# The first product of the last MLP as seven block products with sums of blocks

## The chip, the cores and the metric

The kernel runs on one NeuronCore of a Trainium2 chip. The metric is the device time of one execution in microseconds (us), as the median of several executions. The engines are named as in the profile: PE (TensorE, matmuls), PEld (its weight loads), DVE (VectorE), ACT (ScalarE), POOL (GpSimd), and SP, whose queue issues the loads.

## The reference, cut to what matters

One transformer block on 1024 tokens of width 1024: a mixer of two kinds of sparse attention, cross-attention to a memory, and an MLP, each with a residual sum. All is float32. What the change touches is the MLP:

```python
def _sq_relu_mlp(h, w_ff_in, w_ff_out):
    return jnp.square(jax.nn.relu(h @ w_ff_in)) @ w_ff_out
...
        x = x + _sq_relu_mlp(_rms_norm(x, norm3_g[l]), w_ff_in[l], w_ff_out[l])
```

`w_ff_in` is 1024 x 4096 and `w_ff_out` 4096 x 1024.

## The kernel before, in words

The tokens are eight tiles of 128. The kernel projects them, then runs the attention of each tile while other work (projection of the second half, the memory's keys, the dense part of finished tiles) fills PE's gaps; `together`, `beside` and `merge` interleave these streams by the numbers that they yield. After the attention only dense work is left: `between` (output projection, cross-attention) for tiles 4 and 5 in the pool `dn` and for tiles 6 and 7 in the pool `d2`, merged, and then `mlp(d2, 4, 4, x2s)` for tiles 4 to 7, alone. The functions write the instructions in program order, with tiles from rings of fixed depth (`RINGS`) and PSUM banks by tag (`PSUMS`: S 2, PT 2, PV 1, D 2, M 1). A scheduler then orders the instructions of each engine by a timeline of its own, and each engine runs its queue in that order.

A float32 product is done as three fast ones (type float32r): each operand is split into a high part (a rounding copy) and a low part (the rest), and high x high, low x high and high x low are summed in PSUM. Weights are split by `split_w` (lines 240 to 249): the high part on ACT, the low part on POOL or DVE, two of three on POOL in this stage (`PLAN_TAIL`). `mm` (line 218) records every matmul, so the profile shows all under L218.

`mlp` (line 988) first reads x2 of tiles 4 and 5 back from DRAM (L993), while tiles 6 and 7 are still in SBUF. `norm_T2` (line 289) squares and sums a tile (L293), gets the scale (L229, L231), norms it in halves (L297), transposes it on PE (L274) and splits it into xh and xl (L235, L236). The MLP then runs in eighths, 512 features each (`f4`). In an eighth, for two blocks of 256 features (`f2`), four loads of 256 KB (L254) are split, and each 128 features get 8 x 3 matmuls over all 512 tokens into one bank of S; relu and square follow on ACT (L1020, L1021), the split of the result h on POOL (L1023, L1024). The second product takes, for each half of the output columns (`c`), four loads of 256 KB and for each token tile 4 x 3 matmuls of 512 columns, also into S; DVE adds the result to x2 (L899), and in the last eighth it is stored. The pools `wraw`, `whi` and `wlo` of `d2` have 3, 6 and 6 buffers, `h` has 8.

## Time and profile before

| what | us |
|---|---|
| median of three runs (1859.41 to 1865.53) | 1861.02 |
| the profiled execution | 1861.12 |
| its span on the core | 1859.0 |
| first matmul of the last MLP, after the span's start | 1492.83 |
| last residual sum starts | 1855.28 |
| PE busy, whole span | 1729.4 |

The granted clock of PE has a mean of 0.973 over the span. In a timeline row the first number is the start, the second the duration, then engine, line, operation, tiles and shape; brackets hold the idle time ahead of it and what ended that. In a row of grouped instructions, the numbers behind the bar are the total busy time in us and the mean of one in ns, then the idle time ahead of them. A matmul's own duration is no measure of its cost, since the next one starts before it ends; the steps from start to start are.

### The profile page before, as it was taken

Reading aid. Unit: us, or ns where it says so; the run is one execution under the profiler, and the core shown is the slowest. Engines: PE = TensorE matmul, PEld = TensorE weight load, DVE = VectorE, ACT = ScalarE, POOL = GpSimd, SP = SyncE. Lnnn points to the kernel's source line nnn. Section 1 sums busy time; section 2 is a strip of 40 time slices with the busy share of each in tenths; the row PEclk is TensorE's granted clock in tenths of the full one; section 3 lists DMA queues with packets and bytes.
Section 4 is the critical chain, followed back from the end, with each engine's and each line's share of the span. In section 5 each row is a group of like instructions: output and inputs, shape, how many; then the busy total and the mean of one; then the engine's idle time right before and its main releaser. Section 6 shows DMA issues by size and latency. Waiting matters only on the chain. (4 is left out here: it accounts for less than half of the span.)

```text
span 1859.0 us, 28028 instructions
## 1 busy us (share of the span) xinstructions
PE 1729.4 (93%) x9262; PEld 1467.8 (79%) x9262; DVE 934.9 (50%) x2353; ACT 1077.2 (58%) x2687; POOL 894.7 (48%) x1034
## 2 busy tenths in 40 slices
PE   5996999899989987899998999999898899999999
PEld 5995988678877776688886888888787778788787
DVE  4554766566773786466545565565333332222222
ACT  4444658898697678756984569975223233333332
POOL 2365557455451344466764766664111134444553
PEclk9998998999999998899999999999998999999999
DMA  8225413166226231121221221222773313222232
GB/s 198 71 86 163 98 35 99 65 212 178 90 86 193 88 83 42 46 70 56 77 77 57 67 72 60 64 71 93 241 249 109 116 63 97 91 91 91 91 98 101
DMA packets 180081, 187.50 MB, mean 101 GB/s; under 512 B 34657, under 2 KB 149089, under 8 KB 179937
## 3 DMA queue, kind: packets, MB, share of 16 engines
q1 hardware_dynamic: 172000, 175.23, 31.2%
q0 software_dynamic: 7936, 10.49, 2.1%
q8 instruction: 73, 1.20, 0.3%
q14 instruction: 72, 0.58, 0.1%
HBM read 164.69 MB, written 20.97 MB: 100 GB/s over the span
## 5 line engine op out<-in xcount | busy, mean ns | idle before, releaser
L249 POOL TENSOR_TENSOR wlo<-wraw,whi 128x512 fp32r<-128x512 f32 (+1 forms) x230 | 308.2, 1349 | 322.3 <-ACT whi L244 265.0
L244 ACT ACTIVATE whi<-wraw 128x512 fp32r<-128x512 f32 (+2 forms) x289 | 180.9, 628 | 251.8 <-PE psS L218 150.0
L218 PE MATMUL psD<-whi,xh 128*128 128x256 f32 (+1 forms) x704 | 192.7, 357 | 5.8 <-ACT whi L244 3.5
L218 PE MATMUL psD<-wlo,xh 128*128 128x256 f32 (+1 forms) x704 | 192.5, 354 | 0.8 <-DMA wlo<-in_w_in_dram 0.6
L218 PE MATMUL psD<-whi,h 128*128 128x512 f32 x512 | 177.1, 406 | 9.4 <-POOL h L1024 3.7
L236 DVE TENSOR_TENSOR pl<-psPT,ph 128x512 fp32r<-128x512 f32 (+1 forms) x232 | 141.8, 620 | 62.2 <-ACT ph L235 61.2
L218 PE MATMUL psS<-whi,h 128*128 128x512 f32 x512 | 162.0, 392 | 5.1 <-DVE b L899 5.1
L688 ACT ACTIVATE S<-S,mn 128x128 f32<-128x128 f32 (+7 forms) x192 | 142.8, 745 | 38.9 <-DVE mn L686 38.2
L235 ACT ACTIVATE ph<-psPT 128x512 fp32r<-128x512 f32 (+1 forms) x232 | 122.9, 541 | 57.7 <-PE psPT L703 50.0
L249 DVE TENSOR_TENSOR wlo<-wraw,whi 128x512 fp32r<-128x512 f32 (+1 forms) x59 | 59.4, 1007 | 175.5 <-ACT whi L244 171.8
L218 PEld LDWEIGHTS psD<-whi,xh 128*128 128x128 f32 x704 | 132.7, 195 | 17.2 <-ACT whi L244 3.9
L218 PEld LDWEIGHTS psD<-wlo,xh 128*128 128x128 f32 x704 | 133.6, 195 | 12.7 <-DMA wlo<-in_w_in_dram 1.0
L703 PE MATMUL psPT<-c_ident,S 128*128 128x128 f32 x816 | 133.9, 279 | 10.3 <-POOL S L693 4.7
L693 POOL TENSOR_SCALAR S<-S,sums,gi 128x640 f32<-128x640 f32 (+7 forms) x128 | 107.4, 850 | 68.2 <-DVE sums L691 59.2
L899 DVE TENSOR_TENSOR b<-psS,b 128x512 f32<-128x512 f32 (+1 forms) x80 | 50.0, 636 | 140.9 <-PE psS L218 140.8
L218 PEld LDWEIGHTS psD<-whi,h 128*128 128x128 f32 x512 | 95.8, 190 | 31.6 <-POOL h L1024 5.0
L218 PEld LDWEIGHTS psS<-whi,h 128*128 128x128 f32 x512 | 96.0, 188 | 29.4 <-DVE b L899 9.4
L218 PE MATMUL psS<-K,qh 128*128 128x384 f32 (+3 forms) x288 | 109.2, 383 | 6.6 <-DVE mn L686 2.6
L703 PEld LDWEIGHTS psPT<-c_ident,S 128*128 128x128 f32 x816 | 97.0, 142 | 20.8 <-POOL S L693 8.1
L899 DVE TENSOR_TENSOR b<-psD,b 128x512 f32<-128x512 f32 (+1 forms) x112 | 63.2, 572 | 87.6 <-PE psD L218 76.0
L218 PE MATMUL psD<-xh,wlo 128*128 128x512 f32 x256 | 102.1, 401 | 0.7 <-POOL wlo L249 0.7
L218 PE MATMUL psD<-wlo,h 128*128 128x512 f32 x256 | 102.3, 402 | 0.0
(299 smaller groups left out, 4643.7 us busy)
## 6 DMA issues: line engine op xcount, KB each, us to landing
wraw<-in_w_ff_in_dram SPq DMA_DIRECT2D x128, 256.0 KB, 2.8
wraw<-in_w_ff_out_dram SPq DMA_DIRECT2D x128, 256.0 KB, 2.7
whi<-in_w_out_dram SPq DMA_DIRECT2D x32, 256.0 KB, 5.3
wlo<-in_w_out_dram SPq DMA_DIRECT2D x32, 256.0 KB, 5.2
wraw<-in_w_in_dram SPq DMA_DIRECT2D x24, 256.0 KB, 3.7
q<-st SPq DMA_DIRECT2D x12, 512.0 KB, 2.6
qin<-q SPq DMA_DIRECT2D x44, 128.0 KB, 2.3
x<-in_x_dram SPq DMA_DIRECT2D x8, 512.0 KB, 5.2
```

What stands on the lines that cost most here:

```text
L218: te.matmul(o, a, b, start=start, stop=stop)
L235: s.activation(hi, src, AF.Copy)
L236: v.tensor_tensor(lo, src, hi, op=ALU.subtract)
L244: s.activation(hi, raw, AF.Copy)
L249: (v if l == "v" else g).tensor_tensor(lo, raw, hi, op=ALU.subtract)
L688: s.activation(S, S, AF.Exp, bias=low, scale=-1.0, accum_out=sums[:, hh:hh + 1])
L693: g.tensor_scalar(Ss[hh], Ss[hh], sums[:, hh:hh + 1], 1.0 if gate is None else gate[:, hh:hh + 1], op0=ALU.mult, op1=ALU.mult)
L703: te.transpose(p2[:, j, hh, :], S[:, (c + j) * P:(c + j + 1) * P], ident)
L899: v.tensor_tensor(dst, pt, dst, op=ALU.add)
```

## The change

The last call `mlp(d2, 4, 4, x2s)` becomes `mlp_seven`, with a pool `d3` of its own beside `d2`. The normed tokens, transposed, stand as a 2 x 2 array of blocks B[k][j]: half of the 1024 inputs (k) by half of the 512 tokens (j). The weights of 256 features are a 2 x 2 array A[i][k]: 128 features by half of the inputs. Where the plain way takes eight products of blocks, the new function takes seven, each 128 features x 512 inputs x 256 tokens, of sums of blocks (the Winograd form of Strassen's scheme). The seven sums of token blocks are made and split once (`operand`, R1 to R7); those of the weights for each 256 features (`weight_sum`, four of them; three of the seven are single blocks). Each product is 4 x 3 matmuls of 256 columns. Its results are summed by DVE out of PSUM into `sum` (lines 1138 to 1144 after the change), and relu and square then work on all four blocks at once; h is split as before.

Beside that: loads are 512 KB (L1117, L1159) through a ring of four `raw` tiles, which at first hold B; `whi` and `wlo` in `d2` get 13 buffers each in place of 6, `wraw` of `d2` goes; the second product uses banks of D, S and PT in turn in place of S alone; the MLP's weights are no longer loaded ahead of the raw tiles. The second product's matmuls, the weights' bytes and the stores are the same in number.

```diff
--- before.py
+++ after.py
@@ -37,7 +37,8 @@
     "p1": {"x4": 5, "st": 2, "relu": 4, "wraw": 4, "whi": 6, "wlo": 6, "c8": 4, "c4": 2, "kraw": 5, "pc": 2},
     "p2": {"x4": 3, "st": 1, "relu": 2, "whi": 4, "wlo": 4, "c8": 3, "c4": 1, "kraw": 4, "pc": 2},
     "dn": {"b4": 4, "h": 8, "relu": 2, "wraw": 2, "whi": 4, "wlo": 4},
-    "d2": {"b4": 4, "h": 8, "relu": 2, "wraw": 3, "whi": 6, "wlo": 6},
+    "d2": {"b4": 4, "h": 8, "relu": 2, "whi": 13, "wlo": 13, "sum": 2},
+    "d3": {"raw": 4, "T": 2, "ws": 4},
 }
 PSUMS = {"p1": {"D": 4, "M": 3, "C": 1}, "main": {"S": 2, "PT": 2, "PV": 1, "D": 2, "M": 1}}
 TAGS = {"p1": ("D", "M", "C"), "p2": ("D", "M", "D"), "dn": ("D", "M"), "d2": ("S", "PT")}
@@ -1044,6 +1045,137 @@
                                           x2[t][:, c * 512:(c + 1) * 512])
                     yield 2.6
 
+    def mlp_seven(pool, px, t0, x2s):
+
+
+        x2 = []
+        for t in range(4):
+            if t0 + t not in x2s:
+                x2s[t0 + t] = ring(pool, "b4", [P, DM])
+                nc.sync.dma_start(x2s[t0 + t], x2_dr[t0 + t])
+            x2.append(x2s[t0 + t])
+        add_to = residual_add(x2)
+        gb3 = gain2(pool, W["norm3_g"])
+        B = [[ring(px, "raw", [P, 4, 256]) for j in range(2)] for k in range(2)]
+        for t in range(4):
+            j, ts_ = t // 2, slice(t % 2 * P, t % 2 * P + P)
+            ss = small(pool, "nss", 1)
+            s.activation(ring(px, "T", [P, DM]), x2[t], AF.Square, accum_out=ss)
+            r = rsqrt_of(pool, ss, DM, 1, "n")
+            for k in range(2):
+                xn = ring(pool, "relu", [P, 512])
+                v.scalar_tensor_tensor(xn, x2[t][:, k * 512:k * 512 + 512], r[:, 0:1], gb3[k], op0=ALU.mult, op1=ALU.mult)
+                to_T(pool, xn, [B[k][j][:, :, ts_]], 4)
+            yield 1.0
+
+        R = {}
+
+        def operand(i, x):
+            R[i] = [px.tile([P, 4, 256], F32R, tag=f"R{i}{n}", name=f"R{i}{n}") for n in "hl"]
+            s.activation(R[i][0], x, AF.Copy)
+            v.tensor_tensor(R[i][1], x, R[i][0], op=ALU.subtract)
+
+        def minus(x, y):
+            d = ring(px, "T", [P, 4, 256])
+            v.tensor_tensor(d, x, y, op=ALU.subtract)
+            return d
+        operand(1, B[0][0])
+        t1 = minus(B[0][1], B[0][0])
+        operand(5, t1)
+        operand(2, B[1][0])
+        t2 = minus(B[1][1], t1)
+        operand(6, t2)
+        operand(3, B[1][1])
+        operand(4, minus(B[1][0], t2))
+        operand(7, minus(B[1][1], B[0][1]))
+
+        def split_of(x):
+            hi, lo = ring(pool, "whi", [P, 4, P], F32R), ring(pool, "wlo", [P, 4, P], F32R)
+            split_w(x, hi, lo)
+            return hi, lo
+
+        def product(pt, i, ws):
+            hi, lo = ws
+            xh, xl = R[i]
+            for k in range(4):
+                mm(pt, hi[:, k, :], xh[:, k, :], k == 0, False)
+                mm(pt, lo[:, k, :], xh[:, k, :], False, False)
+                mm(pt, hi[:, k, :], xl[:, k, :], False, k == 3)
+
+        def weight_sum(x, y, op):
+            d = ring(px, "ws", [P, 4, P])
+            v.tensor_tensor(d, x, y, op=op)
+            return d
+
+        for f4 in range(8):
+            hs = []
+            for f2 in range(2):
+                c0 = (f4 * 4 + f2 * 2) * P
+                raw = []
+                for k in range(2):
+                    x = ring(px, "raw", [P, 4, 256])
+                    nc.sync.dma_start(x, W["w_ff_in"][k * 512:k * 512 + 512, c0:c0 + 256].rearrange("(k p) n -> p k n", p=P))
+                    raw.append(x)
+                A = [[raw[k][:, :, i * P:(i + 1) * P] for k in range(2)] for i in range(2)]
+                w1 = split_of(A[0][0])
+                s1 = weight_sum(A[1][0], A[1][1], ALU.add)
+                w5 = split_of(s1)
+                w2 = split_of(A[0][1])
+                s2 = weight_sum(s1, A[0][0], ALU.subtract)
+                w6 = split_of(s2)
+                w3 = split_of(weight_sum(A[0][1], s2, ALU.subtract))
+                w7 = split_of(weight_sum(A[0][0], A[1][0], ALU.subtract))
+                w4 = split_of(A[1][1])
+
+                d = ring(pool, "sum", [P, 7, 256])
+                x, y, w, z = pst("S", [P, 2, 256]), pst("PT", [P, 2, 256]), pst("D", [P, 2, 256]), pst("PV", [P, 256])
+                c1 = small(pool, "c1", 256)
+                product(x[:, 0], 1, w1)
+                s.activation(c1, x[:, 0], AF.Copy)
+                product(x[:, 1], 5, w5)
+                product(y[:, 0], 2, w2)
+                product(y[:, 1], 6, w6)
+                v.tensor_tensor(d[:, 0:7:6], y, c1[:, None, :].to_broadcast([P, 2, 256]), op=ALU.add)
+                product(z, 7, w7)
+                v.tensor_tensor(d[:, 5], z, d[:, 6], op=ALU.add)
+                v.tensor_tensor(d[:, 3:5], x[:, 1:2].to_broadcast([P, 2, 256]), d[:, 5:7], op=ALU.add)
+                product(w[:, 0], 3, w3)
+                product(w[:, 1], 4, w4)
+                v.tensor_tensor(d[:, 1:3], w, d[:, 4:6], op=ALU.add)
+                s.activation(d[:, 0:4], d[:, 0:4], AF.Relu)
+                s.activation(d[:, 0:4], d[:, 0:4], AF.Square)
+                for i in range(2):
+                    r = d[:, 2 * i:2 * i + 2].rearrange("p a n -> p (a n)")
+                    hh, hl = ring(pool, "h", [P, 512], F32R), ring(pool, "h", [P, 512], F32R)
+                    g.tensor_scalar(hh, r, 1.0, 1.0, op0=ALU.mult, op1=ALU.mult)
+                    g.tensor_tensor(hl, r, hh, op=ALU.subtract)
+                    hs.append((hh, hl))
+                yield 9.7
+            for c in range(2):
+                gr = []
+                for k in range(0, 4, 2):
+                    raw = ring(px, "raw", [P, 2, 512])
+                    r0 = (f4 * 4 + k) * P
+                    nc.sync.dma_start(raw, W["w_ff_out"][r0:r0 + 256, c * 512:(c + 1) * 512].rearrange("(k p) n -> p k n", p=P))
+                    for i in range(2):
+                        hi, lo = ring(pool, "whi", [P, 512], F32R), ring(pool, "wlo", [P, 512], F32R)
+                        split_w(raw[:, i, :], hi, lo)
+                        gr.append((hi, lo))
+                for t in range(4):
+                    pt = pst(("D", "S", "PT")[t % 3], [P, 512])
+                    ts_ = slice(t * P, (t + 1) * P)
+                    for f in range(4):
+                        hh, hl = hs[f]
+                        wh, wl = gr[f]
+                        mm(pt, hh[:, ts_], wh, f == 0, False)
+                        mm(pt, hh[:, ts_], wl, False, False)
+                        mm(pt, hl[:, ts_], wh, False, f == 3)
+                    add_to(c, t, pt)
+                    if f4 == 7:
+                        nc.sync.dma_start(out[0, (t0 + t) * P:(t0 + t + 1) * P, c * 512:(c + 1) * 512],
+                                          x2[t][:, c * 512:(c + 1) * 512])
+                    yield 2.6
+
     def pe_stack():
         pe = p1.tile([P, 2, 32], F32R, tag="pe", name="pe")
         pe2 = ring(p1, "relu", [P, 2, 2, 64])
@@ -1111,7 +1243,9 @@
     rest = (w for w in rest if not isinstance(w, tuple))
     merge((rest, REST), (between(d2, 6, 2, x2s, True), 45.0))
     dn_pool.__exit__(None, None, None)
-    drain(mlp(d2, 4, 4, x2s))
+    d3_pool = tc.tile_pool(name="d3", bufs=1, reuse_waits="tile")
+    drain(mlp_seven(d2, d3_pool.__enter__(), 4, x2s))
+    d3_pool.__exit__(None, None, None)
     d2_pool.__exit__(None, None, None)
     ctx.close()
```

## The prediction, made before the changed kernel ran

> **What bounds the kernel now.** I read the page first, then the busy times of the last MLP alone, then the chain of work that ended last.
>
> ```profile
> PE 1729.4 (93%) x9262; PEld 1467.8 (79%) x9262; DVE 934.9 (50%) x2353; ACT 1077.2 (58%) x2687; POOL 894.7 (48%) x1034
> ```
> ```profile
> 1492.83:1855.28 362.45, 357.31 (x1538) 288.60 (x1536) 85.89 (x106) 113.95 (x187) 170.97 (x145) 1.00 0.29 92
> ```
> ```profile
> by line: PE psS L218 96.6%; DVE b L899 2.1%; PE psPT L274 0.3%; issue 0.2%
> ```
>
> The second row is one stretch: its ends (first and last matmul of the last MLP), its length, the busy us of PE, PE's weight loads, DVE, ACT and POOL with their instructions, then PE's granted clock and the DMA. TensorE is busy for 357.31 of the 362.45 us, VectorE for 85.89, ScalarE for 113.95 and GpSimd for 170.97. The chain (from 1492 us on) is nearly all matmuls of line 218, so here a matmul less is time won. A busy matmul is pipelined, so what one costs is the step from one start to the next:
>
> ```profile
> 1599.66 0.40 PE L218 MATMUL psS<-xh,whi 128*128 128x512 f32 x1
> ...
> 1606.39 0.40 PE L218 MATMUL psS<-xl,whi 128*128 128x512 f32 x1
> ...
> 1611.62 0.61 PE L218 MATMUL psS<-whi,h 128*128 128x512 f32 x2
> 1612.80 0.50 PE L218 MATMUL psS<-whi,h 128*128 128x512 f32 x1 [0.56 <-DVE b L899]
> 1613.13 0.39 PE L218 MATMUL psS<-wlo,h 128*128 128x512 f32 x1
> ...
> 1618.60 0.39 PE L218 MATMUL psS<-wlo,h 128*128 128x512 f32 x1
> ```
> ```profile
> PE psS L218 <- DVE b L899: 5.1, 10, 0.6
> ```
>
> First product: 29 steps in 6.73 us, 0.232 us each. Second product: 24 steps in 5.47 us, 0.228 us. Ten times PE waits for the residual sum to clear one of the two S banks: the pair at 1611.62 should be followed at about 1612.08 and is followed at 1612.80, so 0.72 us is lost, 7.2 us in all. An eighth of the MLP has 96 matmuls of each product: 22.3 + 21.9 = 44.2 us. Eight of them and the waits make 360.5 of the 362.45 us; the other 2.0 us is the slow beginning.
>
> **The change part by part.**
>
> *Matmuls.* One eighth had 2 x 2 x 8 x 3 = 96 products of 512 columns; now it has 2 x 7 x 4 x 3 = 168 of 256. The first projection of the kernel runs such 256-column matmuls, each with its own weight load, too:
>
> ```profile
> 28.92 0.28 PE L218 MATMUL psD<-whi,xh 128*128 128x256 f32 x1
> ...
> 30.10 0.29 PE L218 MATMUL psD<-wlo,xh 128*128 128x256 f32 x1
> ...
> 31.56 0.28 PE L218 MATMUL psD<-whi,xh 128*128 128x256 f32 x1
> ...
> 33.26 0.28 PE L218 MATMUL psD<-wlo,xh 128*128 128x256 f32 x1
> ```
>
> 10 steps in 1.18 us (0.118) and 15 in 1.70 us (0.113). I take 0.116, half of 0.232. So 168 x 0.116 = 19.5 us in place of 22.3: **2.78 us less per eighth, 22.3 us in all**; with 0.113 it is 26, with 0.118 it is 20. The 72 more weight loads cost nothing while they lie under the preceding matmul. Their price if that cover is gone is this row:
>
> ```profile
> L218 PEld LDWEIGHTS psS<-wlo,h 128*128 128x128 f32 x256 | 48.1, 188 | 9.7
> ```
>
> *Waits for the S bank.* The second product now rotates over D, S and PT, six banks in place of two: **7.2 us less**; the lower bound is nothing, if new waits stand there.
>
> *Work of the other engines.* Per eighth there are 22 weight splits in place of 16, 8 weight sums, 8 sums of products and 2 copies; relu, square and the split of h keep their size.
>
> ```profile
> L249 POOL TENSOR_TENSOR wlo<-wraw,whi 128x512 fp32r<-128x512 f32 x81 | 107.6, 1335 | 124.7 <-ACT whi L244 123.6
> ...
> L1024 POOL TENSOR_TENSOR h<-relu,h 128x512 fp32r<-128x512 f32 x32 | 44.5, 1391 | 1.8
> L249 DVE TENSOR_TENSOR wlo<-wraw,whi 128x512 fp32r<-128x512 f32 x41 | 43.1, 1050 | 164.1 <-ACT whi L244 164.1
> L899 DVE TENSOR_TENSOR b<-psS,b 128x512 f32<-128x512 f32 x63 | 42.5, 688 | 109.9 <-PE psS L218 109.9
> L1023 POOL TENSOR_SCALAR h<-relu 128x512 fp32r<-128x512 f32 x32 | 20.3, 634 | 62.1 <-ACT relu L1021 62.1
> ```
>
> GpSimd: 14.7 x 1.335 + 4 x (1.391 + 0.634) = 27.7 us. VectorE: 7.3 low parts and 8 weight sums at 1.05, 8 residual sums and 6 product sums at 0.69, 2 small ones at 0.42: 26.6 us. Both are below the 41.4 us of PE, so they bind only through order.
>
> *The order that may bind.* In the built program VectorE's queue puts s1 of the next but one weight block, and before it the four sums of the next block, ahead of the last product sum (after, line 1144). Behind that wait relu, square and GpSimd's two splits of h, which the second product needs. PE meanwhile has 36 matmuls on the two older h blocks: 36 x 0.228 = 8.2 us of cover after the seventh product, and 15 more to the last h. Counting from the start of the first block's products: its seventh ends at 9.7 us; the weights for the next block, whose raw tiles come free when the second product's first weights are split (9.5, behind the fourth product), are there one load of 4.5 us later, at 14 (its row stands below); eight two-input operations of VectorE at 1.05 and four reads of PSUM (10.9 us) end line 1144 at 25.0; relu and square of 1024 elements (1.06 each), then GpSimd's 0.63 + 1.39 + 0.63 + 1.39, end at 31.2. PE reaches that h at 19.5 + 51 x 0.228 = 31.1. Cover and chain are equal. I take 0.7 us of wait for each of the 7 later eighths, **5 us**; bounds 0 (VectorE alone, 0.69 an operation, below) and 2 each (14).
>
> *Start.* Before, the last residual sum and the first matmul stand 13.8 us apart:
>
> ```profile
> 1479.04 0.42 DVE L899 TENSOR_TENSOR b<-psS,b 128x256 f32<-128x256 f32 x1 [1.30 <-PE psS L218]
> 1479.09 1.06 ACT L293 ACTIVATE xh<-b 128x1024 fp32r<-128x1024 f32 x1 [0.28 <-PE psS L218]
> ...
> 1492.83 0.77 PE L218 MATMUL psS<-xh,whi 128*128 128x512 f32 x1
> ```
> ```profile
> L297 DVE SCALAR_TENSOR_TENSOR relu<-b,nr,h 128x512 f32<-128x512 f32 x8 | 5.9, 748 | 2.1 <-POOL nr L231 1.3 <-issue 0.7
> ...
> L899 DVE TENSOR_TENSOR b<-psS,b 128x256 f32<-128x256 f32 x6 | 2.5, 424 | 7.2 <-PE psS L218 7.2
> L249 DVE TENSOR_TENSOR wlo<-wraw,whi 128x512 fp32r<-128x512 f32 x2 | 1.4, 686 | 5.1 <-ACT whi L244 5.1
> ```
> ```profile
> wraw<-in_w_ff_in_dram SPq DMA_DIRECT2D x128, 256.0 KB, 2.8
> ...
> b<-in_x_dram SPq DMA_DIRECT2D x8, 512.0 KB, 4.5
> ```
>
> 256 more elements cost VectorE 0.264 us, so 1024 take about 1.22 (estimate). Now tiles 4 and 5 are normed and transposed inside the product before, where 16 transposes stand among the matmuls behind norms that wait for the tiles' loads; I let that delay it by 2.2 us, so its last sum ends at 1481.7. Then VectorE does in turn: norm of tile 6 (1.5), R1l and R2l (2.4), the wait for tile 7's scale and its norm (2.2); the transposes and copies of tile 7 end at 1488.3. Five operations of 1.22, the first low part (0.69) and two more of 1.22 follow: 1497.5. Only then is the raw tile free that holds the first tokens and is to take the second half of the first weights. The 512 KB load, at 5 us, lands at 1502.6; s1, its high part and its low part (0.7 + 0.63 + 1.34) let the second product go at 1505.3. The first has been done in the gap, the last six take 6 x 1.39 and a slow beginning: 1514.5. Less the 9.7 us that seven products take, that is as if they had begun at 1504.8, **12 us later** (bounds 9 and 16: a load of 2.8 us and no delay, or the double of both). In the first eighth the raw tiles for the second product come late too: the second block's splits end near 1516.5, the load behind them lands at 1521.5, and ScalarE's queue has seven splits, two of them from that load, ahead of the first relu. So relu and square end at 1524.9 and the first h's high part at 1525.5; GpSimd then has two low parts (to 1529.0) ahead of its low part, 1530.4. PE is there at 1514.5 + 9.7 = 1524.2 with ten matmuls that need high parts alone (2.3 us): it waits 1.3, then 2.6 us, and I add 0.6 for each of the two last h: **5 us** (bounds 2 and 8). The 2.0 us of slow beginning lies inside these waits.
>
> *The rest.* Rings of 13 instead of 6 for whi and wlo let the previous stage load earlier, and the MLP's own early loads are gone from that stretch of SP's queue; I cost this at nothing, since PE waits there for norms. If it frees or adds one wait for a load it is 2 us.
>
> **The sum**: -22.3 - 7.2 - 2.0 + 12 + 5 + 5 = -9.5 us. The profiled execution took 1861.1 us (span 1859.0), and the median of the runs shown is 1861.0. So 1851.6.
>
> **Rivals.**
>
> *All of it hidden* (start 9, first eighth 2, later none): -31.5 + 11 = -20.5, 1840.6. For it speaks that both side engines have a third of their time free. Chance 0.2.
>
> *Start and order cost it all* (16 + 8 + 1.5 x 7 = 34.5): 1864, no change. For it: the chain above has no slack. Chance 0.2.
>
> *VectorE and GpSimd in each other's way, slower.* The change triples VectorE's two-input work beside GpSimd.
>
> ```profile
> 1527.44 3.02 POOL L249 TENSOR_TENSOR wlo<-wraw,whi 128x512 fp32r<-128x512 f32 x2 [5.89 <-ACT whi L244]
> ```
> ```profile
> 1528.07 1.22 DVE L249 TENSOR_TENSOR wlo<-wraw,whi 128x512 fp32r<-128x512 f32 x1 [1.33 <-ACT whi L244]
> ```
>
> Alone such an operation took 0.686, here 1.22, and the two on GpSimd took 3.02 and not 2 x 1.29. Eight stand in the chain; if each took d, PE would wait 0.4 + 8 x (d - 1.05). The gain is gone at 2 us, d = 1.25; at 1.5 us it is 4 x 7 = 28 us, with 17 at the start 1875. Against it: the mean in this very stage is 1.05. Chance 0.12. The Trainium skill, Advanced Engine Details and Errata, VectorE Performance Modes, says the second SBUF port is shared and the two engines block each other; full blocking would make d 0.686 + 1.335 = 2.02 and the time about 1904, which the mean of 1.05 denies.
>
> *Weight loads come to light, slower.* 72 more per eighth at 0.188 us are 13.5 us, less 2.78 won: 8 x 10.8 = 86; with -9.2 and +22 for the rest about 1960. Against it: the 0.113 us steps, each with a load. Chance 0.03. In the Trainium skill, TensorE: Matmul & The Clock Gate, Part 3, The mechanism, a weight load overlaps running matmuls only when its row group differs; these use all rows, so by that rule this would be the case, and the rows above disagree with it.
>
> **How the numbers follow.** The forecast has 0.45, with a range of its own of 1845 to 1858. 0.3% is 5.6 us, about what a measurement of this kernel tells from no change. Faster (below 1855.4): 0.2 from the first rival and 0.40 of the forecast. Within: 0.05 of the forecast and 0.2. Slower: 0.15. The range of 1839 to 1867 leaves out the two slow rivals and a little below.
>
> **What would show it.** Right: 256-column matmuls 0.116 us apart; no wait of PE for line 899; the first product's second block beginning near 1504; eighths of 41.4 to 42.5 us from start to start. Wrong: steps above 0.124 us (the loads), PE waiting over 2 us per eighth for GpSimd's h with VectorE's weight sums above 1.25 us, or a start gap above 30 us.

## The result

The changed kernel takes 1849.8 us (median of four runs, 1849.0 to 1853.7), the kernel before beside it 1861.5 (1859.4 to 1865.5): a ratio of 0.9939, with a 95% interval of 0.9917 to 0.9961, or 7 to 15 us less. The forecast was 1851.6. The profiled execution took 1850.3 us, its span is 1848.6.

The busy times of the page, and then those of the stretch from the first to the last product of the last MLP (columns as in the row of before: ends, length, busy us of PE, weight loads, VectorE, ScalarE and GpSimd, PE's granted clock, DMA):

```profile
PE 1713.7 (93%) x9838; PEld 1489.5 (81%) x9838; DVE 1074.3 (58%) x2500; ACT 1110.4 (60%) x2726; POOL 957.7 (52%) x1066
```
```profile
1488.81:1844.80 355.99, 346.56 (x2112) 311.77 (x2112) 221.25 (x255) 146.01 (x225) 240.70 (x181) 0.97 0.31 99
```

PE's busy time falls by 15.7 us, VectorE's rises by 139.4, nearly all of it here (85.89 before). In this stretch PE was busy for all but 5.1 us before; now 9.4 are idle. The waits of PE for line 899 (now 900) are gone. From 1505 us on it waits for these, in all, times and longest:

```profile
PE psS L219 <- ACT c L1134: 3.7, 1, 3.7
PE psS L219 <- DVE sum L1141: 0.9, 3, 0.3
PE psD L219 <- DVE sum L1144: 0.3, 1, 0.3
```

The first is in the first eighth. Once this is over, PE's own rows in the fourth eighth's first block read:

```profile
1639.90 0.28 PE L219 MATMUL psD<-R3h,whi 128*128 128x256 f32 x1
...
1641.34 0.28 PE L219 MATMUL psD<-R4h,whi 128*128 128x256 f32 x1
...
1642.78 0.28 PE L219 MATMUL psS<-R1h,whi 128*128 128x256 f32 x1
```

Twelve steps in 1.44 us, twice: 0.120 us a step and not 0.116. An eighth's first product so takes 168 x 0.120 = 20.16 us, 2.11 less than the 22.27 of before, where 2.78 were forecast.

The start is the other end of the account. All of PE's waits from the first product to the second product of the first eighth:

```profile
1488.81 0.58 PE L219 MATMUL psS<-R1h,whi 128*128 128x256 f32 x1 [5.55 <-ACT whi L245]
1489.69 0.58 PE L219 MATMUL psS<-R1h,wlo 128*128 128x256 f32 x1 [0.30 <-DVE wlo L250]
1496.02 0.58 PE L219 MATMUL psS<-R5h,whi 128*128 128x256 f32 x1 [3.62 <-ACT whi L245]
1497.38 0.58 PE L219 MATMUL psS<-R5h,wlo 128*128 128x256 f32 x1 [0.25 <-POOL wlo L250]
1517.61 0.58 PE L219 MATMUL psS<-R5h,whi 128*128 128x256 f32 x1 [3.74 <-ACT c L1134]
```

The first block of products takes from 1488.81 to 1508.63, 19.8 us for 84 x 0.12 = 10.1 of work. VectorE's weight sums show why; here those of the first blocks, in order:

```profile
1494.62 0.69 DVE L1107 TENSOR_TENSOR ws<-raw 128x512 f32<-128x512 f32 x1 [0.24 <-DMA raw<-in_w_ff_in_dram]
1495.34 0.69 DVE L1107 TENSOR_TENSOR ws<-ws,raw 128x512 f32<-128x512 f32 x1
1496.07 1.80 DVE L1107 TENSOR_TENSOR ws<-raw,ws 128x512 f32<-128x512 f32 x1
1497.79 1.77 DVE L1107 TENSOR_TENSOR ws<-raw 128x512 f32<-128x512 f32 x1
```

The first waits for the weights. Those were loaded into tiles that the token blocks had held, and their two loads were issued only here:

```profile
1484.33 0.38 SPq L1117 DMA_DIRECT2D raw<-in_w_ff_in_dram  x1
...
1490.84 0.38 SPq L1117 DMA_DIRECT2D raw<-in_w_ff_in_dram  x1
```

The second landed at 1494.59, just ahead of the first sum. From 1496.05 on GpSimd works as well, and an operation of 0.69 us takes 1.8.

**How the kernels are compared below.** One profiled run differs from the next in the stages that all kernels share. So each trace is read from a mark, placed in the stage ahead of the last MLP: the twelve 128-column matmuls psS<-h.

```profile
1451.07 1.64 PE L219 MATMUL psS<-h 128*128 128x128 f32 x12
```

In the kernel before they begin at 1457.44. S2 is the first matmul of the second product in the second eighth, behind which six and a half even eighths follow; the end is that of the last matmul. All lengths in us:

| kernel | mark to S2 | S2 to end | together | median, its ratio to before |
|---|---|---|---|---|
| before | 104.3 | 293.5 | 397.8 | 1861 to 1863 |
| changed | 117.0 | 276.7 | 393.7 | 1849.8, 0.9939 |
| e1_banks | 103.7 | 286.2 | 389.9 | 1854.1, 0.9956 |
| e2_halves | 100.7 | 296.2 | 396.9 | 1858.4, 0.9984 |
| e3_eight | 101.7 | 290.9 | 392.5 | 1853.0, 0.9956 |
| e4_seventh_early | 115.4 | 276.1 | 391.4 | 1850.4, 0.9942 |
| e5_preload | 105.5 | 278.5 | 384.0 | 1846.4, 0.9902 |
| e6_rings | 104.4 | 292.3 | 396.7 | 1860.3, 0.9994 |
| e8_lows_dve | 109.6 | 274.4 | 383.9 | 1843.7, 0.9900 |
| e9_sums_twice | 122.7 | 307.1 | 429.8 | 1892.4, 1.0163 |
| e10_plain_block | 105.8 | 280.8 | 386.6 | 1848.3, 0.9925 |
| e11_plain_eighth | 101.9 | 278.6 | 380.4 | 1840.9, 0.9885 |
| e12_own_fourth | 101.1 | 278.0 | 379.1 | 1843.1, 0.9897 |
| e13_own_dve | 99.0 | 273.8 | 372.9 | 1831.9, 0.9835 |

The changed kernel gains 16.8 us in the even part and gives 12.7 back in the first eighth and what lies around it. The traces' sums and the medians differ by some microseconds, since the stretch ahead of the mark and the scatter of the runs are in the medians alone.

### The profile page after: what moved, and what is told of

The parts are those of the page before. It is cut to its first block, busy times and chain, and to the rows that moved or that the text cites. A ratio compares the mean times of both kernels' runs of the same rounds, so it can differ in the third digit from the quotient of the medians.

```text
span 1848.6 us, 29327 instructions
## 1 busy us (share of the span) xinstructions
PE 1713.7 (93%) x9838; PEld 1489.5 (81%) x9838; DVE 1074.3 (58%) x2500; ACT 1110.4 (60%) x2726; POOL 957.7 (52%) x1066
## 4 chain that ended last, share of the span: by engine, by line
PE 44%; issue 6%; DVE 6%; POOL 5%; DMA 5%; ACT 4%; SPq 1%; ACTq 0%; POOLq 0%; DVEq 0%
PE psD L219 23%; PE psS L219 11%; PE psPT L219 4%; PE psPV L219 3%; POOL wlo L250 3%; PE psPT L704 2%; DVE ws L1107 1%; DMA wraw<-in_w_ff_in_dram 1%; DMA raw<-in_w_ff_in_dram 1%; DMA wraw<-in_w_ff_out_dram 1%; ACT dmask L645 1%; POOL S L694 1%; DMA whi<-in_w_out_dram 1%; ACT whi L245 1%; POOL h L1025 0%
## 5 line engine op out<-in xcount | busy, mean ns | idle before, releaser
L219 PE MATMUL psD<-whi,h 128*128 128x512 f32 x768 | 266.0, 403 | 10.5 <-DVE b L900 3.6
L250 POOL TENSOR_TENSOR wlo<-wraw,whi 128x512 fp32r<-128x512 f32 x145 | 195.1, 1355 | 155.0 <-ACT whi L245 143.4
L219 PEld LDWEIGHTS psD<-whi,h 128*128 128x128 f32 x768 | 144.8, 191 | 44.2 <-DVE b L900 4.5
L900 DVE TENSOR_TENSOR b<-psD,b 128x512 f32<-128x512 f32 (+1 forms) x144 | 85.2, 598 | 130.0 <-PE psD L219 127.7
L219 PE MATMUL psD<-wlo,h 128*128 128x512 f32 x384 | 153.1, 400 | 0.0
L245 ACT ACTIVATE whi<-wraw 128x512 fp32r<-128x512 f32 (+1 forms) x161 | 100.0, 625 | 59.2 <-DMA wraw<-in_w_ff_in_dram 16.3
L245 ACT ACTIVATE whi<-raw 128x512 fp32r<-128x512 f32 x112 | 69.6, 628 | 106.7 <-PE psD L219 82.7
L250 POOL TENSOR_TENSOR wlo<-raw,whi 128x512 fp32r<-128x512 f32 x74 | 103.1, 1400 | 52.5 <-ACT whi L245 51.3
L232 POOL TENSOR_TENSOR nr<-nms,mhalf 128x1 f32<-128x1 f32 x26 | 14.9, 572 | 179.5 <-DVE nms L230 179.4
L219 PE MATMUL psD<-xh,wlo 128*128 128x512 f32 x256 | 101.9, 401 | 0.6 <-POOL wlo L250 0.6
L219 PE MATMUL psD<-xh,whi 128*128 128x512 f32 x256 | 100.8, 402 | 0.8 <-ACT xh L236 0.8
```

Source lines behind the costliest of these rows:

```text
L219: te.matmul(o, a, b, start=start, stop=stop)
L232: g.tensor_tensor(r, ms, mhalf[:, 0:1].to_broadcast([P, w]), op=ALU.pow)
L245: s.activation(hi, raw, AF.Copy)
L250: (v if l == "v" else g).tensor_tensor(lo, raw, hi, op=ALU.subtract)
L900: v.tensor_tensor(dst, pt, dst, op=ALU.add)
```

## Experiments

**The banks alone** (e1_banks, on the kernel before):

```diff
-                    pt = pst(TAGS[pool.name][0], [P, 512])
+                    pt = pst(("D", "S", "PT")[t % 3] if pool.name == "d2" else TAGS[pool.name][0], [P, 512])
```

> The kernel before, with one thing of the change alone: in the last MLP the second product's sums go over the banks D, S and PT in turn, where they all went to S and PT in the kernel before; the products stay as they were. Theory of the prediction: the ten waits of 0.72 us for the eviction of the bank S go and nothing takes their place, 7.2 us less than the kernel before (1861.5 - 7.2 = 1854.3, a ratio of 0.996). Rival: TensorE then waits for the next thing (a split of weights, h), and the time stays within 2 us of the kernel before. The two are told apart by the time and by PE's waits for line 900 after 1505 us.

1854.1 us, a ratio of 0.9956 (0.9939 to 0.9973), 7.9 less between mark and end, and PE waits for nothing after 1490 us. The prediction's 7.2 holds. By size this term of the change is two thirds of its whole result, and it needs no products by blocks. (In the kernel before all these sums go to S alone, not to S and PT as the expectation has it, and the line is 899.)

**The step of 256 columns** (e2_halves, on the kernel before):

```diff
-                    for k in range(8):
...
-                        mm(pt, wh[:, fs], xh[:, k, :], k == 0, False)
+                    wide = 256 if pool.name == "d2" else nt * P
+                    for j in range(0, nt * P, wide):
+                        cs = slice(j, j + wide)
+                        for k in range(8):
...
+                            mm(pt[:, cs], wh[:, fs], xh[:, k, cs], k == 0, False)
```

> The kernel before, with the last MLP's first product done in two halves of 256 columns, each with all its weight loads again: 192 matmuls of 256 columns for each eighth of the hidden units in place of 96 of 512, and nothing else. The prediction's price of 0.116 us a step gives 192 x 0.116 = 22.3 us, what 96 x 0.232 took: no change (within 2 us). The price read in the changed kernel, 0.120, if it belongs to every such step that has a weight load of its own, gives 192 x 0.120 = 23.0, 0.77 more in each eighth and 6.1 in all: 1867.6 (ratio 1.0033). If the 0.120 comes from something else of the change (other engines at work beside it), the steps here show 0.116. Rival, the loads exposed at 0.19 us each: 14 us more in each eighth, some 1975.

1858.4 us, 0.9984 (0.9972 to 0.9996). The 192 steps of an eighth take 22.67 us here (1627.57 up to the second product at 1650.24), 0.118 each: neither of the two prices. From S2 on it is 2.7 us slower than before, as 0.4 in each eighth says. That it is not slower in all comes from the start, 3.6 us shorter: matmuls of the first half of the tokens stand among the last transposes there. The loads are not exposed, and the time decides for neither theory: it is 3 us below the kernel before.

**Eight products in the new frame** (e3_eight, on the changed kernel):

```diff
-                w1 = split_of(A[0][0])
-                s1 = weight_sum(A[1][0], A[1][1], ALU.add)
...
+                ws = [[split_of(A[i][k]) for k in range(2)] for i in range(2)]
...
+                for i in range(2):
+                    x = pst(("S", "PT")[i], [P, 2, 256])
+                    for j in range(2):
+                        product(x[:, j], j, ws[i][0], True, False)
+                        product(x[:, j], 2 + j, ws[i][1], False, True)
```

> The changed kernel's frame (its pools, loads, order, blocks of 256 tokens, banks in turn) with the eight plain block products in place of the seven and without any of the sums of blocks: the same result by the ordinary rule. Steps per eighth 192 in place of 168, so by the step of 0.120 it loses 24 x 0.120 = 2.9 us in each eighth, 23.0 in all; it gains the waits of the eighths that the sums cause (5.6 us over the eight in the changed kernel) and part of the start (the sums of blocks before the first products, and the wait of 3.7 us in the first eighth: together 4 to 8). Theory: 1849.8 + 23.0 - 5.6 - 6 = 1861, between 1857 and 1868. Rival, that the sums of blocks eat the eighth product's worth and the gain came from the banks and the frame alone: 1850 or less.

1853.0 us, 0.9956 (0.9939 to 0.9973): below what the theory said, and not told apart from the changed kernel by the intervals. It is also above the rival's 1850. The trace tells why. From S2 on, where six first products lie, the seven products win 14.2 us over the eight (276.7 against 290.9), 2.4 in each eighth of the 2.9 that 24 steps of 0.120 are worth. Up to S2 they lose 15.3 (117.0 against 101.7), although two first products lie there and should win 5.8. So the sums cost 21 us up to there, where I had put 6, and that eats the whole gain.

**What the start waits for.** First, the operand that holds back the second weight load, made earlier (e4_seventh_early, on the changed kernel):

```diff
         t1 = minus(B[0][1], B[0][0])
         operand(5, t1)
+        operand(7, minus(B[1][1], B[0][1]))
```

> The changed kernel with the operand of the seventh product made right behind the first difference of blocks (a third buffer of T for it), so that the last reader of the blocks B, whose buffers the second weight load takes, is done earlier; all else is the same. Theory: the second block's load starts some 4 us earlier, the wait of 3.74 us for the raw split at 1517.6 and part of the gap before the second block go: 1849.8 - 3.7 = 1846, at best 1844. Rival: the loads already come in time for what VectorE and ScalarE can do there, the wait moves to the next split, and the time stays within 1.5 us of the changed kernel (1848.3 to 1851.3). It may cost up to 1 us where the first products wait one more operation for their operands.

1850.4 us, 0.9942 (0.9927 to 0.9957): the rival. The wait for line 1134 is as long as it was, and so is the one before the first product:

```profile
1492.00 0.58 PE L219 MATMUL psS<-R1h,whi 128*128 128x256 f32 x1 [5.80 <-ACT whi L245]
...
1520.30 0.58 PE L219 MATMUL psS<-R5h,whi 128*128 128x256 f32 x1 [3.73 <-ACT c L1134]
```

Of the loads for the second product, the second landed 3.4 us earlier than in the changed kernel (counted from the mark), but the third, whose splits the copy of line 1134 stands behind, only 0.8.

Then the first weights loaded early, into tiles that are free (e5_preload, on the changed kernel):

```diff
+        early = []
+        for k in range(2):
+            x = ring(pool, "sum", [P, 7, 256])[:, 0:4]
+            nc.sync.dma_start(x, W["w_ff_in"][k * 512:k * 512 + 512, 0:256].rearrange("(k p) n -> p k n", p=P))
+            early.append(x)
```

> The changed kernel with one thing else: the weights of the very first block are loaded at the head of the last MLP into the two buffers of 'sum', which are free there, and not into buffers of the blocks B that the operands have to leave first. From the last residual sum of the stage before to the first product of the second eighth the kernel before took 60.4 us (1479.04 to 1539.45), the changed kernel 71.05 (1475.57 to 1546.62). Theory of the prediction (the start is late because the second raw tile of weights comes free only behind VectorE's operands): the first products, whose operands are ready at 1478.5, stand among the last transposes, the weight sums are done before the operands, and the stretch shrinks by 6 to 9 us to some 63; 1842 to 1844 in all. Rival: VectorE's fourteen operations of 1.22 us for operands bind in any case; the stretch shrinks by 1 to 3 us, 1847 to 1849.

1846.4 us, 0.9902 (0.9873 to 0.9931). The time lies between the two expectations, and its interval (1838 to 1849) leaves both open; the trace decides. Between mark and S2 it is 11.5 us shorter than the changed kernel, so the load was the larger part of the late start, as the prediction said; from S2 on it is 1.8 longer. The stretch that the expectation named cannot be read as it was meant, since the last residual sum stands at another place in VectorE's order here. (VectorE has eleven operations of 1.22 us for the operands, not fourteen: seven low parts and four sums; three of the seven operands are single blocks.) Late now are the last operand and h:

```profile
1505.64 0.38 PE L219 MATMUL psPV<-R7l,whi 128*128 128x256 f32 x1 [1.88 <-DVE R7l L1081]
1519.56 0.80 PE L219 MATMUL psD<-whi,h 128*128 128x512 f32 x1 [3.81 <-POOL h L1156]
```

Then also the first block, and the first eighth, by eight plain products, which need no sums (e10_plain_block; e11_plain_eighth has 2 in place of 1):

```diff
+                if f4 * 2 + f2 < 1:
+                    ws = [[split_of(A[i][k]) for k in range(2)] for i in range(2)]
...
+                        for i in range(2):
+                            product(xs[i][:, j], (1, 0)[j], ws[i][0], True, False)
+                            product(xs[i][:, j], 2 + j, ws[i][1], False, True)
```

> As the kernel with the early first weights, and the first block of hidden units is done by the ordinary eight products, which need the four blocks of tokens as they are and no sums; the operands of the other products are made beside them, and the first half of the tokens can begin before the second half is transposed. Costs 24 steps of 0.120 = 2.9 us/2 = 1.4 us for the block. Theory (the start is bound by sums of blocks on VectorE): the stretch from the last residual sum to the second eighth falls from 71 to about 58 to 60, what the kernel before took, and the time to 1838 to 1841. Rival: VectorE's operations come due in the second block instead, beside GpSimd at 1.7 us each, and only half of it is won: 65, 1844.

> As the kernel before this one in the list, with the ordinary eight products for both blocks of the first eighth. It costs 1.4 us more on TensorE, and takes four weight sums and four of the product sums from VectorE where its operands are made. Theory: if the second block of the kernel with one plain block waits over 1.4 us for VectorE, this is the faster of the two, near 1838; if not, it is the slower by 1.4 us, below what the comparison can tell, and the trace's waits of the first eighth decide.

One block: 1848.3 us, 0.9925 (0.9901 to 0.9948), no gain over the early weights alone and worse than the rival's 1844. Its second block waits 3.9 us for a low part on VectorE and 1.9 for a high part: the sums come due there. The whole eighth: 1840.9, 0.9885 (0.9862 to 0.9908), and 6.2 us less between mark and end than with one block; the 5.8 us of waits less the 1.4 of the added products gave 4.4. It is 3 us above the 1838 of the expectation. Mark to S2 is now what eight products took in the same frame (101.9 and 101.7), so nearly all that the sums cost there is won back, and the kernel is 12 us below the one with eight products (1840.9 against 1853.0, by the traces 380.4 against 392.5).

The next wait there was, by the trace's names, for the seventh operand (R7), whose buffers the fourth block of tokens held. Buffers of its own, and rings of 11 to make room (e12_own_fourth):

```diff
-            t = i or 7
+            t = i
```

> The kernel with the early first weights and the ordinary eight products for the whole first eighth, with buffers of its own for the operand of the fourth block of tokens, which had shared those of the seventh product's operand and held that back until the first eighth's products were done; the rings of weights' parts go from 13 to 11 to make room. There TensorE waited 1.5 + 2.3 us for the seventh operand. Theory: those waits go, 3 to 4 us: 1837. Rival: the rings of 11 cost as much, or the next operand is as late: 1841.

1843.1 us, 0.9897 (0.9879 to 0.9915): no gain that can be told. The two waits are still there, as long as before (1.5 and 2.3), and now the trace names the operand of the fourth block itself (R0): it had borne the shared name R7 before, and the shared buffer was not their cause. In the even part nothing is won or lost (278.0 and 278.6).

**Slack in the eighths** (e9_sums_twice, on the changed kernel):

```diff
             v.tensor_tensor(d, x, y, op=op)
+            v.tensor_tensor(d, x, y, op=op)
```

> The changed kernel with each of the eight weight sums of an eighth done twice over by VectorE, the second time into the same tile: some 8 x 1.2 us more on VectorE for each eighth, 26.6 to about 36.5 busy of 41.8; the result is the same. The prediction put cover and chain in the eighths equal at 31 us (no slack). By that, the four to five sums that stand in the chain ahead of the last sum of products, doubled, make TensorE wait 5 us more in each of seven eighths: +35 us, 1885. Rival (the chain has slack, since the waits in the changed kernel come to 5.6 us in all and stand in three eighths only): under 1 us in each eighth, below +8, 1850 to 1858. If GpSimd slows as well, its own low parts come late and the time rises past 1885.

1892.4 us, 1.0163 (1.0136 to 1.0190). Six eighths from S2 on take 47.5 us each in place of 42.5: 5 us each, the number of the theory without slack. VectorE is not full, 32.5 to 35.1 us busy in three stretches of 47.5. The waits lie where the chain was put, behind a sum of products (line 1142 here is 1141 of the changed kernel):

```profile
PE psS L219 <- DVE sum L1142: 17.9, 6, 5.3
```

With two smaller rows that is 20.1 us of waits from S2 on, 3.4 an eighth. The rest comes behind them: for 23.9 us of these six eighths together PE had half its clock, which is some 12 us of work lost (estimate from these two figures). In the first of the three stretches (the last but two of the columns is the clock):

```profile
1580.96:1628.50 47.54, 43.16 (x251) 38.30 (x250) 32.52 (x41) 18.35 (x28) 28.10 (x22) 0.93 0.30 89
```

**GpSimd and VectorE side by side** (e8_lows_dve, on the changed kernel):

```diff
+    plan["w"] = ("av",)
     d3_pool = tc.tile_pool(name="d3", bufs=1, reuse_waits="tile")
```

> The changed kernel with all the low parts of the last MLP's weights on VectorE, where two thirds were on GpSimd, which keeps only the splits of h. Theory A (VectorE and GpSimd are in each other's way: VectorE's two-input operation takes 0.69 alone and 1.0 to 1.33 beside GpSimd): with GpSimd busy some 10 us of 42, VectorE's operations fall to some 0.75 to 0.8; 22 low parts, 8 sums and its reads of PSUM come to 31 to 33 us of each eighth, a little more than now, and the time stays within 3 us of the changed kernel or is up to 5 us less. Theory B (1.2 is what such an operation costs in this stage whoever else works): 22 x 1.0 + 8 x 1.2 + 9 = 41 us of 41.8, VectorE becomes the bound and the chain, which has no slack, costs over 5 us in each eighth: 1890 or more.

1843.7 us, 0.9900 (0.9884 to 0.9916). The rows of VectorE from 1590 to 1840 us, first of the changed kernel (low parts and weight sums: busy us, mean ns), then of this one:

```profile
L1107 DVE TENSOR_TENSOR ws<-raw 128x512 f32<-128x512 f32 x20 | 26.6, 1331 | 26.3 <-DMA raw<-in_w_ff_in_dram 11.6 <-POOL wlo L250 11.4 <-POOL h L1150 3.2
L250 DVE TENSOR_TENSOR wlo<-raw,whi 128x512 fp32r<-128x512 f32 x27 | 26.4, 979 | 17.3 <-ACT whi L245 17.3
L250 DVE TENSOR_TENSOR wlo<-ws,whi 128x512 fp32r<-128x512 f32 x14 | 17.1, 1223 | 3.0 <-ACT whi L245 2.8
```
```profile
L250 DVE TENSOR_TENSOR wlo<-raw,whi 128x512 fp32r<-128x512 f32 x78 | 63.6, 821 | 9.9 <-ACT whi L245 9.7
L250 DVE TENSOR_TENSOR wlo<-ws,whi 128x512 fp32r<-128x512 f32 x40 | 29.8, 755 | 5.7 <-ACT whi L245 5.7
L1107 DVE TENSOR_TENSOR ws<-raw 128x512 f32<-128x512 f32 x20 | 18.0, 902 | 11.1 <-DMA raw<-in_w_ff_in_dram 11.0
```

VectorE makes 118 low parts where it made 41, and they are shorter in the mean (0.76 to 0.82 us), as are the weight sums (0.90 of the kind shown). What it costs in all, in the same 41.5 us of both, first of the changed kernel and then of this one (after the ends and the length come the busy us of PE, weight loads, VectorE, ScalarE and GpSimd):

```profile
1591.00:1632.50 41.50, 41.50 (x264) 37.59 (x263) 26.77 (x32) 17.16 (x28) 29.41 (x23) 1.00 0.32 102
```
```profile
1591.00:1632.50 41.50, 41.50 (x263) 37.68 (x262) 33.20 (x46) 17.94 (x28) 9.88 (x8) 1.00 0.31 102
```

Fourteen operations more cost VectorE 6.4 us and spare GpSimd 19.5. Theory A is shown, with a gain of 6 us, a little past its upper end. By the trace it is 2.3 us from S2 on and 7.4 up to S2, where the first block's sums now take 0.68.

Not every operation of VectorE is slower beside GpSimd. In the changed kernel those with one input in PSUM, such as the last product sum, keep their 0.69 us in the same 250 us in which the others, with both inputs in SBUF, go to 0.98 to 1.33 in the mean. From 1440 us on, no 128x512 sum with an input in PSUM took over 0.70 in any of the fourteen traces; the others took up to 1.85.

```profile
L1144 DVE TENSOR_TENSOR sum<-psD,sum 128x512 f32<-128x512 f32 x12 | 8.2, 683 | 7.1 <-PE psD L219 7.1
```

Where both have operations with two inputs in SBUF without a break, as in the first block of the changed kernel from 1497 to 1508 us, their ends alternate, and each engine starts its next about 1.70 us after its last. Alone, VectorE's follow each other at 0.60 in e8_lows_dve and GpSimd's at 1.25 here. First GpSimd, then VectorE:

```profile
1502.36 1.74 POOL L250 TENSOR_TENSOR wlo<-raw,whi 128x512 fp32r<-128x512 f32 x1
1504.05 1.75 POOL L250 TENSOR_TENSOR wlo<-ws,whi 128x512 fp32r<-128x512 f32 x1
```
```profile
1499.48 1.77 DVE L250 TENSOR_TENSOR wlo<-ws,whi 128x512 fp32r<-128x512 f32 x1
1501.18 1.76 DVE L1107 TENSOR_TENSOR ws<-raw 128x512 f32<-128x512 f32 x1
```

**The best version** is e12_own_fourth (early weights, plain first eighth, rings of 11) with all low parts on VectorE (e13_own_dve):

> The same with all the low parts of the last MLP's weights on VectorE. If theory A holds for the changed kernel with that edit, this one takes off some of the 5 us of waits that are left in the eighths: 1832 to 1838. If theory B holds, it is over 1870.

1831.9 us, 0.9835 (0.9821 to 0.9850), 18 less than the changed kernel: just below the range given. Its eighths are 41.98 us from start to start, with no wait in them.

**The rings of the stage before** (e6_rings, on the kernel before):

```diff
-    "d2": {"b4": 4, "h": 8, "relu": 2, "wraw": 3, "whi": 6, "wlo": 6},
+    "d2": {"b4": 4, "h": 8, "relu": 2, "wraw": 3, "whi": 10, "wlo": 10},
```

> The kernel before with rings of 10 in place of 6 for the high and low parts of weights in the last two stages (13 do not fit beside its other buffers); nothing else. In the profiles so far the stage before ended between 1472.8 and 1482.1 us, 1479.0 in the kernel before and 1475.6 in the changed kernel. Theory of the prediction (the deeper rings are worth nothing there, 2 us at most): within 2 us of the kernel before. Rival: they let that stage's loads run ahead, 3 to 4 us less, and that is the part of the changed kernel's 11 us that the last MLP's own trace (7.0 us from the last residual sum to the end) does not show.

1860.3 us, 0.9994 (0.9983 to 1.0004): within the 2 us of the theory.

## Why the prediction came out right, point by point

**Matmuls, -22.3: the direction right, the size wrong.** The step that failed is "I take 0.116": these blocks run at 0.120, so the term is 2.11 x 8 = 16.9 us, 5.4 short and below the bound of 20 worked out from a step of 0.118. The bounds came from another stage's rows, and the even part's own price was in none of them. That the 72 more weight loads stay hidden was right; whether the last 0.004 us of a step belong to them stays open. The Trainium skill, TensorE: Matmul & The Clock Gate, Part 3, The mechanism, says in its list that a load overlaps running matmuls only where the row group differs (the paragraph above the list also names the background weight buffer); steps of 0.120 us, each with a load of 0.19 us, disagree with the list here too.

**Waits for the S bank, -7.2: right**, 7.9 by the trace of the banks alone.

**Order, +5: right in kind, too large.** The last six steps from eighth to eighth are 42.46 us in the mean and would be 41.98 without a wait, as in e13_own_dve: 2.9 us in all. That cover and chain are nearly equal was right, and the doubled sums show it: 5 us in each eighth. Weight sums of up to 1.33 us, past the 1.25 that was to be the end of the gain, did not do it: the other operations of that chain stayed at 0.98 to 1.22 (low parts) and 0.69 (reads of PSUM).

**Start, +12: right, with its reason, but two errors in it cancel.** The last residual sum stands 24.5 us behind the mark, 21.6 before: the transposes delay it by 2.9, where 2.2 stood. The second block begins 33.1 us behind that sum (1475.57 to 1508.63); by the working it was 1481.3 (that sum's start; 1481.7 is its end) to 1514.5, or 33.2. ("Near 1504", the sign named for it, was wrongly copied: it is when the first block would have had to begin.) Together, 33.1 + 2.9 less the 13.8 of before and the 10.1 that the block needs, 12.1. Inside it the weights landed 19.0 us behind that sum's start and not 21.3, and from there the block took 14.0 us and not 11.9, with most of VectorE's sums at 1.8 and GpSimd's low parts at 1.7 us in place of 0.7 and 1.39, and with PE at half its clock until 1503. The early weights show that the late load is the cause of most of it.

**First eighth, +5 less 2.0: too small, and with another wait.** From the first product to the first matmul of the second product it takes 36.8 us (1488.81 to 1525.65) for 168 x 0.120 = 20.2: 16.7 lost, 9.7 of them in the first block, which the start counts, 6.9 in the second. Another 0.4 is lost before the next eighth (42.4 us in place of 41.98). Before, 1.7 were lost at this place (24.0 for 22.3). So the term is 5.7 where 3 stood. The waits for h that the prediction put there came to 0.1 us. PE waited 3.7 us for the copy of the first product's bank (the last row), and then ran 6 us at half its clock. On ScalarE the copy stood behind seven splits, two of them of a load that had come late, and behind the first block's relu, which waited for VectorE's last product sum (L1144), itself behind a low part of that load:

```profile
1513.27 1.15 ACT L245 ACTIVATE whi<-raw 128x512 fp32r<-128x512 f32 x2 [0.74 <-DMA raw<-in_w_ff_out_dram]
1516.23 1.06 ACT L1145 ACTIVATE sum<-sum 128x1024 f32<-128x1024 f32 x1 [1.81 <-DVE sum L1144]
1517.20 0.36 ACT L1134 ACTIVATE c<-psS 128x256 f32<-128x256 f32 x1
```

**The rest, at nothing: wrong.** In the last 80 matmuls ahead of the mark, the same in all fourteen traces, the ten kernels with the new frame take 15.0 to 15.3 us, the four with the old frame 16.7 to 18.1 (before 18.1, changed 15.0). The prediction named the place, "the MLP's own early loads are gone from that stretch of SP's queue", and cost it at nothing, "since PE waits there for norms". In the kernel before PE also waited there for a load, and its next eight matmuls took 3.5 us at half its clock:

```profile
1447.17 0.63 PE L274 MATMUL psM<-c_ident,relu 128*128 128x128 f32 x4 [1.01 <-DMA relu<-xo]
```
```profile
1441.18 0.38 SPq L254 DMA_DIRECT2D wraw<-in_w_ff_in_dram  x1
1441.65 1.06 SPq L972 DMA_DIRECT2D xo<-relu  x2
1444.49 0.32 SPq L978 DMA_DIRECT2D relu<-xo  x1
```

The changed kernel has no weight load ahead of those stores, which land in 1.7 us in place of 2.4 to 2.8; PE does not wait there, and the eight matmuls take 1.8 us:

```profile
1442.49 0.63 PE L275 MATMUL psM<-c_ident,relu 128*128 128x128 f32 x4
```

The deeper rings alone do not do it (e6_rings has 17.6). No run takes those loads away and nothing else, so this cause is read from the rows and not tested.

**The sum.** From the mark on the trace shows -4.1 and not -9.5: 5.4 more for the step, 2.7 for the first eighth, 0.1 for the start, 2.1 less for the order, 0.7 less for the banks. The 80 matmuls ahead of the mark make it -7.2, at the edge of the 7 to 15 us that the measurement gives. The other 3.3 us by which the mark lies earlier in the changed kernel's profile (1451.07 and 1457.44) are scatter as far as the traces tell: at the 7000th matmul, at 1329 us in the kernel before, no engine's order differs yet between the kernels, and the traces already stand between 2.8 us ahead of it and 4.1 behind. So the forecast of -9.5 is close to the measured -11.6 in part by luck: the terms that it added up came to -4.1, one that it cost at nothing gave 2 to 3 us, and the rest can't be told from scatter.

**Rivals.** "All of it hidden" (1840.6) has the time that the kernel reaches once the start is mended, 1840.9 with early weights and a plain first eighth, but by another sum: its products were to win 22.3 and not 16.9. "Start and order cost it all" put 16, 8 and 10.5 for start, first eighth and order where 12.1, 7.4 and 2.9 came (7.4 is the 5.7 above and the 1.7 of before). "VectorE and GpSimd in each other's way" is a real mechanism that did not decide the sign: taking GpSimd's low parts away won 6 us. The Trainium skill, Advanced Engine Details and Errata, VectorE Performance Modes, says that GpSimd's instructions and those of VectorE that use two ports block each other at a shared port. The rows agree for VectorE's operations with two inputs in SBUF: where both engines have such work, they take turns (the rows under e8_lows_dve). The prediction's 2.02 for that case added two durations, which overlap a little. That the means are 0.98 to 1.33 denies no blocking; GpSimd is at work 71% of the time. "Weight loads come to light" is refuted.

## What to carry to other kernels

Fewer multiplications bring what the even part shows only if the operands of the first step are there in time: in this kernel that meant to begin the stage with the plain form, which needs no prepared sums, and to load its first weights into tiles that nothing must leave first. Take a step's price from the very shape and place in which it will run, since 3% on 1344 steps were half of the result. When a change takes loads out of a queue, look which waits of the stage before hang on that queue. And before an engine's free time is given more work, see what its neighbour does meanwhile: low parts moved from GpSimd (71% busy) to VectorE (64%) became shorter, and the kernel with them.

## What the runs showed of the hardware

The 256-column matmuls on the blocks run at 0.120 us a step at full granted clock, those of e2_halves, on halves of a 512-column tile, at 0.118; half of a 512-column one is 0.116. Nothing here says what makes the difference.

A wait of 3.7 us cost PE more than itself. The stretch behind it has half the granted clock (last but two of the columns) for 6.1 us, 28 matmuls at 0.21 us:

```profile
1517.60:1523.70 6.10, 6.09 (x28) 6.09 (x29) 3.56 (x4) 2.46 (x4) 5.44 (x6) 0.50 0.78 242
```

That is 2.7 us more, and the waits at the start have the same behind them (0.50 to 0.55 from 1490 to 1504). The waits of 0.2 to 0.3 us in the even part left the clock at 1.00; this is an eighth with one of them:

```profile
1568.07:1610.65 42.58, 42.24 (x266) 38.11 (x265) 27.67 (x34) 18.25 (x28) 30.06 (x24) 1.00 0.35 110
```
